# Low parts of a weight piece's sums in one operation, sums made ahead in three operations, and two norms' roots moved into the softmax

## The chip, the cores and the metric

The kernel runs on one core of a Trainium2 chip. The core's engines run side by side, each one through its own instructions in their order: TensorE (PE: matmuls; PEld: its weight loads), VectorE (DVE), ScalarE (ACT), GpSimd (POOL) and SyncE (SP). An instruction waits by semaphores for what other engines or DMA transfers must have finished. The metric is the time of one execution in device microseconds (us); lower is better.

## What is computed

The reference is one layer of a streaming encoder in float32, on 256 tokens with 2048 features. Cut to its frame:

```python
x = x + 0.5 * swiglu(rms_norm(x, ffn1_norm[l]), ffn1_w_up[l], ffn1_w_down[l])
h = rms_norm(x, mix_norm[l]); proj = h @ w_in[l]
...                                   # HGRN2 and RG-LRU branches, gates, w_out
x = x + cross_attention(rms_norm(x, xattn_norm[l]), rms_norm(mem, mem_norm[l]), wq, wkv, wo)
x = x + 0.5 * swiglu(rms_norm(x, ffn2_norm[l]), ffn2_w_up[l], ffn2_w_down[l])
return rms_norm(x, final_norm)

def swiglu(h, w_up, w_down):
    gate, up = jnp.split(h @ w_up, 2, axis=-1)
    return (jax.nn.silu(gate) * up) @ w_down
```

In the cross attention, 4 heads of 512 features attend to 256 memory tokens: scores = q k^T * 512^-0.5, softmax over the memory tokens, times v, then wo. An RMS norm multiplies a token's row by 1/sqrt(mean of squares + eps), here called its root, and each feature by a gain. The root of a token is one number for the whole row, so it can be applied before or after a product with a weight. The feed-forward width is 5632, so each of the two feed-forward parts reads an up weight of 2048 x 11264 and a down weight of 5632 x 2048.

## The kernel before

**Pieces.** All weights come as pieces of 128 x 2048 numbers (1 MB). SP issues the load of a piece into a tile `raw`; the products read it as a high part and a low part, both in the reduced form that TensorE multiplies fast. `split` (L137 to L139) makes them: ScalarE copies the piece to the high part `h`, and VectorE subtracts that from the piece, which gives the low part `l`. The activations are split in the same way (`xh`, `xl`). A product then consists of three: h by xh (L547), h by xl (L548) and l by xh (L550, in the function `three`). In a feed-forward piece all h matmuls come ahead of the l matmuls.

**Fewer matmuls by sums.** For most up pieces (kind "fast") the kernel multiplies sums of the four 128x512 blocks of a piece in place of some of the blocks, so that 7 products do the work of 8. In `prepare`, VectorE makes the sums `td` from `raw`: one operation of 128x1024 (L285), then one of 128x512 (L287) and one more (L288), each of which needs the one before. The blocks that are used as they are get split as 128x1536 (`h`, `l`), and `td` gets split into `th` and `tl` in two halves of 1024 columns: two ScalarE copies (L138) and two VectorE subtractions (L139, 128x1024). In the first feed-forward part `td` and `tl` lie in a pool `wide` of three tiles; in the second `td` lies in a tile of the raw pools (so the profile shows it as raw), and `tl` in `wide`, of two tiles.

Other kinds are "fast added" (the low part of the 1536 columns is made by a ScalarE copy with the sign turned and a POOL DMA that adds the weight to it, L293 to L295), "added" (the same for a whole piece, L254 to L263), "plain" (one split of 128x2048), and "ready": there `td` isn't computed but loaded from a tile `t` in DRAM.

**Sums made ahead.** For the "ready" pieces of the second feed-forward part, 58 of them, `make_ahead` (L191 to L202) runs in the middle of the kernel: POOL issues the load of the piece into `prep`, VectorE makes the sums in place with four subtractions of 128x512 (L200), and POOL issues the store to `t`. `beside` (called for every piece) says after which piece the next such load, or its sums and store, are put into the instruction stream.

**Order.** The stages follow each other: first feed-forward part (up to about 690 us in the profile), input projection and branches, gates and output (up to about 1356), q and k of the cross attention, scores, v and o (up to about 1740), second feed-forward part (up to 2417). A feed-forward cycle is 8 up pieces, and 4 down pieces of an earlier group; between them stand the activation (L580, L581) and transposes (L588) that give `hidop`, the operand of the down pieces. `weights` prepares two pieces ahead of the one in use; pools of three raw, three h and three l tiles limit how far that goes (a new load waits until the last reader of the tile is done). The order of the instructions within each engine is decided by a scheduler when the kernel is built: it simulates the engines and places what is ready. Only the first eight pieces have an order written by hand. So a change in an operation's cost or form can also change the order of other instructions.

**Norms of q and k.** In the loop over q's 16 tiles (L1088), `summed` (L347 to L355) adds the two partial results of a product (L352) and, where `by=` is given, multiplies the sum by a [128, 256] tile (L354). For q that tile is `by_feature(sq3.rstd_tokens())`: the roots as a column per token are turned into a row by two VectorE products with the identity, one matmul with ones, and one ScalarE copy; then it is scaled by 512^-0.5. For k it is `rmem` (L1105), which comes from `sqm.rstd()`. `scores` (L1110) multiplies q and k (L1118, L1119), adds the parts, takes the maximum over the memory tokens (L1122), turns its sign (L1123), and lets ScalarE take Exp with that as bias and the sum as a second result (L1124).

Of the kernel before, what the change touches and what calls it, by code (L numbers as in the profile page):

```python
# [8 lines left out]
F32 = mybir.dt.float32  # L9
F32R = mybir.dt.float32r  # L10
ACT = mybir.ActivationFunctionType
ALU = mybir.AluOpType

P = 128
# [8 lines left out]
HD = D // HEADS  # L23
# [54 lines left out]
def block_kernel(ctx: ExitStack, tc: tile.TileContext, xT, xin, memT, vec, gfin, bgate, lruw, wu1, wd1, win, wv,  # L78
                 wg, wab, wout, wq, wk, wvm, wo, wu2, wd2, out_):
    nc = tc.nc  # L80
    pe, dve, act, sp = nc.tensor, nc.vector, nc.scalar, nc.sync
# [23 lines left out]
    def slot(dt=F32, name="slot"):  # L105
        return slots.tile([P, 1024], dt, name=name, tag="slot")

    def t1(name="t1"):
        return scoped["tmp"].tile([P, T], F32, name=name, tag="t1")

    def bank(name="acc"):
        return psum.tile([P, 512], F32, name=name, tag="acc")
# [18 lines left out]
    x = [xt[k // 4][:, (k % 4) * T:(k % 4 + 1) * T] for k in range(KT)]  # L131
    ident = col("ident", 0, P)

    done = {}


    def split(h, l, raw):  # L137
        done["high"] = act.activation(h, raw, ACT.Copy).ins  # L138
        done["low"] = dve.tensor_tensor(out=l, in0=raw, in1=h.bitcast(F32), op=ALU.subtract).ins  # L139

    def split_tiles():
        return hp.tile([P, 2048], F32R, name="h", tag="h"), lp.tile([P, 2048], F32R, name="l", tag="l")
# [49 lines left out]
    def make_ahead(src, to):  # L192

        t = scoped["prep"].tile([P, 2048], F32, name="prep", tag="prep")
        nc.gpsimd.dma_start(t, src)
        yield
        b = [t[:, i * 512:(i + 1) * 512] for i in range(4)]
        with tc.issue_after(done["low"]):
            for o, x, y in ((1, 0, 1), (0, 0, 2), (2, 2, 1), (3, 3, 2)):
                dve.tensor_tensor(out=b[o], in0=b[x], in1=b[y], op=ALU.subtract)  # L200
        nc.gpsimd.dma_start(to, t)
        yield  # L202

# [39 lines left out]
    def raw_tile():  # L243

        if "raw2" in scoped and next(loads) % 5 > 2:
            return scoped["raw2"].tile([P, 2048], F32, name="raw2", tag="raw2")
        return rawp.tile([P, 2048], F32, name="raw", tag="raw")
# [10 lines left out]
    def prepare(src, kind, cuts=1):  # L258

        if kind == "added":  # L260
            raw, l = begun.pop(0)
            h = hp.tile([P, 2048], F32R, name="h", tag="h")
            done["high"] = act.activation(h, raw, ACT.Copy).ins  # L263
            return h, l
        raw = raw_tile()
        n = 2048 // cuts
        if kind == "plain":
            h, l = split_tiles()
            for a in range(0, 2048, n):
                sp.dma_start(raw[:, a:a + n], src[:, a:a + n])  # L270
                split(h[:, a:a + n], l[:, a:a + n], raw[:, a:a + n])
            return h, l
        if kind == "ready":
            src, t = src
            sp.dma_start(raw[:, 512:], src[:, 512:])
            td = raw_tile()
            sp.dma_start(td, t)
        else:
            sp.dma_start(raw, src)
            if "raw2" in scoped:  # L280
                td = raw_tile()
            else:
                td = scoped["wide"].tile([P, 2048], F32, name="td", tag="wide")
            two = [v[:, a:a + 1024].rearrange("p (i n) -> p i n", i=2) for v, a in ((td, 0), (raw, 512))]
            dve.tensor_tensor(out=two[0], in0=raw[:, None, :512].broadcast_to([P, 2, 512]), in1=two[1],  # L285
                              op=ALU.subtract)
            dve.tensor_tensor(out=td[:, 1024:1536], in0=raw[:, 1024:1536], in1=td[:, :512], op=ALU.subtract)  # L287
            dve.tensor_tensor(out=td[:, 1536:], in0=raw[:, 1536:], in1=td[:, 1024:1536], op=ALU.subtract)  # L288
        h, l = split_tiles()
        if kind != "fast added":  # L290
            split(h[:, 512:], l[:, 512:], raw[:, 512:])
        else:
            act.activation(l[:, 512:], raw[:, 512:], ACT.Copy, scale=-1.0)  # L293
            nc.gpsimd.dma_start(l[:, 512:], src[:, 512:], accum_op=ALU.add)
            done["high"] = act.activation(h[:, 512:], raw[:, 512:], ACT.Copy).ins  # L295
        th = hp.tile([P, 2048], F32R, name="h", tag="h")
        if "wide" in scoped:
            tl = scoped["wide"].tile([P, 2048], F32R, name="tl", tag="wide")
        else:
            tl = lp.tile([P, 2048], F32R, name="tl", tag="l")  # L300
        for a in (0, 1024):
            split(th[:, a:a + 1024], tl[:, a:a + 1024], td[:, a:a + 1024])
        return (h, l), (th, tl)

    def product(xs, *ws, late=()):
# [41 lines left out]
    def summed(acc, out=None, by=None):  # L347

        lo = t1("lo")
        act.activation(lo, acc[:, T:], ACT.Copy)  # L350
        out = t1("sum") if out is None else out
        dve.tensor_tensor(out=out, in0=acc[:, :T], in1=lo, op=ALU.add)  # L352
        if by is not None:
            dve.tensor_tensor(out=out, in0=out, in1=by, op=ALU.mult)  # L354
        return out  # L355
# [103 lines left out]
    def by_feature(r):  # L459

        diag = t1("diag")
        for t in range(2):
            dve.tensor_scalar(out=diag[:, t * P:(t + 1) * P], in0=ident, scalar1=r[:, t:t + 1], scalar2=None,
                              op0=ALU.mult)
        acc = bank()
        pe.matmul(acc[:, :T], ones, diag, start=True, stop=True)
        o = small.tile([P, T], F32, name="rstd", tag="rstd", bufs=2)
        act.activation(o, acc[:, :T], ACT.Copy)
        return o
# [310 lines left out]
    def heads(t):  # L780
        return t.rearrange("p (h t) -> p h t", h=4)
# [291 lines left out]
    xs3, sq3 = Operands(), TokenSquares()  # L1073
# [12 lines left out]
    qs = Operands()  # L1086
    ms, sqm = Operands(), Squares()
    for m in range(KT):  # L1088
        acc = two_ahead(xs3.tiles, "q", m, 0, late)
        if m == 0:  # L1090
            rstd = by_feature(sq3.rstd_tokens())
            dve.tensor_scalar(out=rstd, in0=rstd, scalar1=HD ** -0.5, scalar2=None, op0=ALU.mult)
        qs.add(summed(acc, by=rstd))
        for i in range(2 * m, 2 * m + 2) if m < 4 else (m + 4,) if m < 12 else ():
            if i % 4 == 0:
                mt = slot(name="mem")
                sp.dma_start(mt, memT[:, i * T:(i + 4) * T])
            mk = heads(mt)[:, i % 4]
            ms.add(mk, col("mem_norm", i))
            sqm.add(mk)  # L1100
    ks = Operands()
    for m in range(KT):
        acc = two_ahead(ms.tiles, "k", m, 0)
        if m == 0:
            rmem, rmtok = sqm.rstd(), sqm.rstd_tokens()  # L1105
        ks.add(summed(acc, by=rmem))

    probs = {}

    def scores(h):  # L1110
        p = slot(name="p")
        pv = p.rearrange("p (t m) -> p t m", t=4)
        for t in range(2):
            acc = bank()
            for j in range(4):
                d = h * 4 + j
                a, b = t * P, T + t * P
                pe.matmul(acc, qs.tiles[d][:, a:a + P], ks.tiles[d], start=(j == 0), stop=False)  # L1118
                pe.matmul(acc[:, :T], qs.tiles[d][:, b:b + P], ks.tiles[d][:, :T], start=False, stop=(j == 3))  # L1119
            s = summed(acc, out=pv[:, t])  # L1120
            st = small.tile([P, 4], F32, name="st", tag="st", bufs=4)
            dve.tensor_reduce(out=st[:, 0:1], in_=s, axis=mybir.AxisListType.X, op=ALU.max)  # L1122
            dve.tensor_scalar(out=st[:, 1:2], in0=st[:, 0:1], scalar1=-1.0, scalar2=None, op0=ALU.mult)  # L1123
            act.activation(s, s, ACT.Exp, bias=st[:, 1:2], accum_out=st[:, 2:3])  # L1124
            dve.reciprocal(out=st[:, 3:4], in_=st[:, 2:3])
            dve.tensor_scalar(out=s, in0=s, scalar1=st[:, 3:4], scalar2=None, op0=ALU.mult)
            yield
        acc = bank()
        for mt in range(2):
            for t in range(2):  # L1130
                pe.transpose(acc[:, mt * T + t * P:][:, :P], pv[:, t, mt * P:(mt + 1) * P], ident)
        ps = slot(F32R, "ps")
        psv = ps.rearrange("p (m t) -> p m t", m=2)
        av = acc.rearrange("p (m t) -> p m t", m=2)
        act.activation(psv[:, :, :T], av, ACT.Copy)
        dve.tensor_tensor(out=psv[:, :, T:], in0=av, in1=psv[:, :, :T].bitcast(F32), op=ALU.subtract)
        probs[h] = ps
        yield
# [3 lines left out]
    for g in range(4):  # L1142
# [4 lines left out]
        for t in range(2):  # L1147
            s = slot(F32R, "vs")
# [8 lines left out]
    for h in range(HEADS):  # L1157
        for j in range(4):
            acc = bank()
            for t in range(2):  # L1160
                ps = probs[h][:, t * 512:(t + 1) * 512]
                s = vs[h, t]
# [153 lines left out]
```

## Time and profile before

| | us |
|---|---|
| median of 3 runs | 2428.28 |
| lowest and highest run | 2426.31 and 2430.49 |
| span of the profiled execution | 2425.5 |

No separate time is given for the profiled execution, so its span is the only number for it; it lies 2.8 us below the median.

How to read the profile's rows: a group row holds the line, engine, operation, what it writes and reads with shapes, and the count; then busy time and mean duration of one (ns), then the idle time of the engine right before these instructions and what ended it. A timeline row holds start and duration in us, engine, line, operation, names and shapes, a count where several follow each other, and in brackets the idle time before it with the releaser. A row of waits holds the waiting instruction, what it waited for, and the total, the number and the longest of the waits. A row of the chain holds start and duration of a step of the work that ended last. In a row of a window, after the stretch and its length, come the busy time of PE, PEld, DVE, ACT and POOL with their counts, the clock that TensorE was granted (1.00 is full), the share of the DMA engines and GB/s. Matmuls are pipelined: the records of two in a row overlap, so a matmul's record is longer than the step from one to the next.

### The profile page before, as it was taken

To read this page: it belongs to the slowest core of one execution; us is meant where nothing else is said; L and a number is where in the kernel's file an instruction comes from. 1 tells how busy PE (TensorE), PEld (TensorE's weight loads), DVE (VectorE), ACT (ScalarE), POOL (GpSimd) and SP (SyncE) were. 2 spreads that over 40 slices of the span, in tenths; PEclk is the share of its full clock that TensorE was granted. 3 is DMA by queue.
4 is the path that set the end of the run, shared out by engine and by line. 5 is a ranking of instruction groups with operands and counts; after the bars stand their busy time and mean duration, and the time that the engine had idled before them with its cause. 6 is when DMAs were issued, how large, how long until landed. Compare 5 with 4: busy or idle time off the path is not lost.

```text
span 2425.5 us, 30763 instructions
## 1 busy us (share of the span) xinstructions
PE 2409.3 (99%) x12139; PEld 2013.6 (83%) x12139; DVE 2025.6 (84%) x2260; ACT 1455.0 (60%) x1485; POOL 102.2 (4%) x166
## 2 busy tenths in 40 slices
PE   9999999999999999999999999999999999999998
PEld 8888888888788888888888888888888788888887
DVE  7999999998876868779776788777789999999995
ACT  8567677777664454476434555445676666666664
POOL 0000000000000000000000000000000000000000
PEclk9999999999999999999999999999999999999999
DMA  7579999988858776778989889977798878787873
GB/s 294 195 229 287 272 272 270 275 269 268 266 183 323 268 289 241 294 289 323 346 313 349 310 332 354 335 272 263 264 343 308 285 266 293 273 286 276 294 273 144
DMA packets 102385, 684.31 MB, mean 282 GB/s; under 512 B 11361, under 2 KB 11617, under 8 KB 29281
## 3 DMA queue, kind: packets, MB, share of 16 engines
q1 hardware_dynamic: 78192, 518.68, 57.5%
q0 software_dynamic: 23328, 162.54, 22.4%
q8 instruction: 95, 1.56, 0.2%
q10 hardware_dynamic: 720, 1.13, 0.1%
q14 instruction: 50, 0.40, 0.0%
HBM read 619.39 MB, written 62.91 MB: 281 GB/s over the span
## 4 chain that ended last, share of the span: by engine, by line
PE 91%; DVE 3%; DMA 3%; ACT 1%; issue 1%; ACTq 0%; DVEq 0%; SPq 0%
PE acc L547 16%; PE acc L548 16%; PE acc L550 16%; PE acc L313 11%; PE acc L338 8%; PE acc L341 8%; PE acc L339 8%; PE acc L316 6%; DMA raw<-wd 2%; DVE tl L139 1%; ACT h L138 1%; DVE l L139 1%; PE acc L588 1%; PE acc L477 1%; DMA t<-prep 0%
## 5 line engine op out<-in xcount | busy, mean ns | idle before, releaser
L138 ACT ACTIVATE h<-raw 128x2048 fp32r<-128x2048 f32 (+3 forms) x578 | 870.5, 1531 | 620.2 <-PE acc L339 189.6
L139 DVE TENSOR_TENSOR l<-raw,h 128x2048 fp32r<-128x2048 f32 (+2 forms) x406 | 837.3, 2065 | 187.6 <-ACT h L138 186.1
L547 PE MATMUL acc<-h,xh 128*128 128x512 f32 x1241 | 485.2, 392 | 2.7 <-ACT h L138 2.4
L548 PE MATMUL acc<-h,xl 128*128 128x512 f32 x1241 | 483.0, 390 | 0.0
L338 PE MATMUL acc<-h,ops 128*128 128x512 f32 x832 | 326.8, 393 | 0.0
L339 PE MATMUL acc<-h,ops 128*128 128x512 f32 x832 | 324.5, 390 | 0.0
L547 PEld LDWEIGHTS acc<-h,xh 128*128 128x128 f32 x1241 | 233.3, 188 | 56.2 <-ACT h L138 8.0
L547 PE MATMUL acc<-h,hidop 128*128 128x512 f32 x704 | 276.5, 393 | 2.3 <-ACT h L138 2.2
L313 PE MATMUL acc<-ops,h 128*128 128x512 f32 x1152 | 278.2, 393 | 0.0
L548 PE MATMUL acc<-h,hidop 128*128 128x512 f32 x704 | 274.8, 390 | 0.0
L548 PEld LDWEIGHTS acc<-h,xl 128*128 128x128 f32 x1241 | 233.3, 188 | 47.5
L313 PEld LDWEIGHTS acc<-ops,h 128*128 128x128 f32 x1152 | 211.7, 188 | 41.6
L139 DVE TENSOR_TENSOR tl<-raw,h 128x1024 fp32r<-128x1024 f32 x172 | 203.7, 1220 | 14.9 <-ACT h L138 14.5
L341 PE MATMUL acc<-l,ops 128*128 128x512 f32 x832 | 205.8, 389 | 0.0
L550 PE MATMUL acc<-l,hidop 128*128 128x512 f32 x704 | 189.3, 389 | 0.0
L138 ACT ACTIVATE h<-td 128x1024 fp32r<-128x1024 f32 x126 | 131.3, 1057 | 92.9 <-PE acc L548 42.3
L341 PEld LDWEIGHTS acc<-l,ops 128*128 128x128 f32 x832 | 156.2, 188 | 32.4
L338 PEld LDWEIGHTS acc<-h,ops 128*128 128x128 f32 x832 | 156.2, 188 | 32.2
L339 PEld LDWEIGHTS acc<-h,ops 128*128 128x128 f32 x832 | 156.3, 188 | 31.5
L139 DVE TENSOR_TENSOR tl<-td,h 128x1024 fp32r<-128x1024 f32 x126 | 152.0, 1220 | 31.2 <-ACT h L138 31.0
L200 DVE TENSOR_TENSOR prep<-prep 128x512 f32<-128x512 f32 x232 | 159.7, 689 | 20.9 <-DMA prep<-wu 17.1
L550 PE MATMUL acc<-l,xh 128*128 128x512 f32 x645 | 176.4, 389 | 0.0
(242 smaller groups left out, 2739.4 us busy)
## 6 DMA issues: line engine op xcount, KB each, us to landing
raw<-wu SPq DMA_DIRECT2D x114, 1024.0 KB, 6.3
raw<-wd SPq DMA_DIRECT2D x88, 1024.0 KB, 6.3
prep<-wu POOLq DMA_DIRECT2D x58, 1024.0 KB, 7.8
t<-prep POOLq DMA_DIRECT2D x58, 1024.0 KB, 7.8
raw<-t SPq DMA_DIRECT2D x58, 1024.0 KB, 6.9
raw<-wu SPq DMA_DIRECT2D x58, 768.0 KB, 5.0
raw<-win SPq DMA_DIRECT2D x40, 1024.0 KB, 4.8
raw<-wg SPq DMA_DIRECT2D x32, 1024.0 KB, 6.1
```

The costliest lines, as they stand in the source:

```text
L138: done["high"] = act.activation(h, raw, ACT.Copy).ins
L139: done["low"] = dve.tensor_tensor(out=l, in0=raw, in1=h.bitcast(F32), op=ALU.subtract).ins
L200: dve.tensor_tensor(out=b[o], in0=b[x], in1=b[y], op=ALU.subtract)
L313: pe.matmul(acc, h[:, k * P:(k + 1) * P], xs[k], start=k == 0, stop=False)
L316: done["product"] = pe.matmul(acc[:, :T], l[:, k * P:(k + 1) * P], xs[k][:, :T], start=False, stop=k == KT - 1).ins
L338: pe.matmul(accs[t], x[:, t * P:][:, :P], h[j], start=first and j == 0, stop=False)
L339: pe.matmul(accs[t], x[:, T + t * P:][:, :P], h[j], start=False, stop=False)
L341: done["product"] = pe.matmul(accs[t], x[:, t * P:][:, :P], l[j], start=False, stop=last and j == 3).ins
L477: pe.transpose(acc[:, z * T + t * P:][:, :P], tile[:, t * 512 + (2 * y + z) * P:][:, :P], ident)
L547: pe.matmul(acc, ah, bh, start=start, stop=False)
L548: pe.matmul(acc, al, bh, start=False, stop=False)
L550: pe.matmul(acc, ah, bl, start=False, stop=stop)
```

## The change

1. The sums' low part: `td` is still copied to `th` in two halves by ScalarE, but `tl` comes from one VectorE subtraction of 128x2048 in place of two of 128x1024. It needs both halves of `th`. This holds for every piece with sums, 149 in all.
2. The sums made ahead: the first two of the four subtractions become one of 128x(2x512), whose first operand is block 0, read twice, whose second operand is blocks 1 and 2, and whose results go to blocks 1 and 0, in that order. Two of 128x512 follow. This holds for the 58 pieces made ahead.
3. The roots: q's and k's tiles are no longer multiplied by anything. q's root with 512^-0.5 stays a column per token, and is used as the scale of Exp and in the product that makes its bias; `by_feature` isn't called. k's root `rmem` multiplies each score tile (8 of them, 128x256).

```diff
@@ -194,10 +194,12 @@
         t = scoped["prep"].tile([P, 2048], F32, name="prep", tag="prep")
         nc.gpsimd.dma_start(t, src)
         yield
-        b = [t[:, i * 512:(i + 1) * 512] for i in range(4)]
+        b = t.rearrange("p (i n) -> p i n", i=4)
         with tc.issue_after(done["low"]):
-            for o, x, y in ((1, 0, 1), (0, 0, 2), (2, 2, 1), (3, 3, 2)):
-                dve.tensor_tensor(out=b[o], in0=b[x], in1=b[y], op=ALU.subtract)
+            dve.tensor_tensor(out=b[:, 1::-1], in0=b[:, :1].broadcast_to([P, 2, 512]), in1=b[:, 1:3],
+                              op=ALU.subtract)
+            for o in (2, 3):
+                dve.tensor_tensor(out=b[:, o], in0=b[:, o], in1=b[:, o - 1], op=ALU.subtract)
         nc.gpsimd.dma_start(to, t)
         yield
 
@@ -299,7 +301,8 @@
         else:
             tl = lp.tile([P, 2048], F32R, name="tl", tag="l")
         for a in (0, 1024):
-            split(th[:, a:a + 1024], tl[:, a:a + 1024], td[:, a:a + 1024])
+            done["high"] = act.activation(th[:, a:a + 1024], td[:, a:a + 1024], ACT.Copy).ins
+        done["low"] = dve.tensor_tensor(out=tl, in0=td, in1=th.bitcast(F32), op=ALU.subtract).ins
         return (h, l), (th, tl)
 
     def product(xs, *ws, late=()):
@@ -1088,9 +1091,9 @@
     for m in range(KT):
         acc = two_ahead(xs3.tiles, "q", m, 0, late)
         if m == 0:
-            rstd = by_feature(sq3.rstd_tokens())
-            dve.tensor_scalar(out=rstd, in0=rstd, scalar1=HD ** -0.5, scalar2=None, op0=ALU.mult)
-        qs.add(summed(acc, by=rstd))
+            rtok = sq3.rstd_tokens()
+            dve.tensor_scalar(out=rtok, in0=rtok, scalar1=HD ** -0.5, scalar2=None, op0=ALU.mult)
+        qs.add(summed(acc))
         for i in range(2 * m, 2 * m + 2) if m < 4 else (m + 4,) if m < 12 else ():
             if i % 4 == 0:
                 mt = slot(name="mem")
@@ -1103,7 +1106,7 @@
         acc = two_ahead(ms.tiles, "k", m, 0)
         if m == 0:
             rmem, rmtok = sqm.rstd(), sqm.rstd_tokens()
-        ks.add(summed(acc, by=rmem))
+        ks.add(summed(acc))
 
     probs = {}
 
@@ -1117,11 +1120,12 @@
                 a, b = t * P, T + t * P
                 pe.matmul(acc, qs.tiles[d][:, a:a + P], ks.tiles[d], start=(j == 0), stop=False)
                 pe.matmul(acc[:, :T], qs.tiles[d][:, b:b + P], ks.tiles[d][:, :T], start=False, stop=(j == 3))
-            s = summed(acc, out=pv[:, t])
+            s = summed(acc, out=pv[:, t], by=rmem)
             st = small.tile([P, 4], F32, name="st", tag="st", bufs=4)
             dve.tensor_reduce(out=st[:, 0:1], in_=s, axis=mybir.AxisListType.X, op=ALU.max)
-            dve.tensor_scalar(out=st[:, 1:2], in0=st[:, 0:1], scalar1=-1.0, scalar2=None, op0=ALU.mult)
-            act.activation(s, s, ACT.Exp, bias=st[:, 1:2], accum_out=st[:, 2:3])
+            r = rtok[:, t:t + 1]
+            dve.tensor_scalar(out=st[:, 1:2], in0=st[:, 0:1], scalar1=r, scalar2=-1.0, op0=ALU.mult, op1=ALU.mult)
+            act.activation(s, s, ACT.Exp, bias=st[:, 1:2], scale=r, accum_out=st[:, 2:3])
             dve.reciprocal(out=st[:, 3:4], in_=st[:, 2:3])
             dve.tensor_scalar(out=s, in0=s, scalar1=st[:, 3:4], scalar2=None, op0=ALU.mult)
             yield
```

## The prediction

> **What bounds the kernel now.** I read the page's first part, the chain of work, then the waits of TensorE, the windows by stage and, where a wait stands, the timeline around it.
>
> ```profile
> span 2425.5 us, 30763 instructions
> PE 2409.3 (99%) x12139; PEld 2013.6 (83%) x12139; DVE 2025.6 (84%) x2260; ACT 1455.0 (60%) x1485; POOL 102.2 (4%) x166
> PE 91%; DVE 3%; DMA 3%; ACT 1%; issue 1%; ACTq 0%; DVEq 0%; SPq 0%
> ```
>
> ```profile
> 11.14 1.81 PE acc L550 x8
> ```
>
> The chain is TensorE for 91%. Its matmuls of 512 columns follow each other at 1.81 / 8 = 0.2265 us, so nothing is won inside its work, only in its gaps. The waits put those in few places:
>
> ```profile
> PE acc L547 <- ACT h L138: 4.6, 5, 2.0
> ...
> PE acc L892 <- DVE k L912: 0.9, 1, 0.9
> ```
>
> Five waits for a high part cost 4.6 us; they all stand where a feed-forward cycle passes from its last up piece to its first down piece. (From start to start a gap is some 0.16 us longer than its idle time, since a matmul's record outlasts its turn.) VectorE is second, and close to full in the feed-forward parts:
>
> ```profile
> 60.00:250.00 190.00, 190.00 (x850) 156.89 (x849) 182.10 (x190) 122.55 (x102) 6.74 (x8) 1.00 0.74 239
> 1905.00:1930.00 25.00, 22.40 (x89) 17.07 (x88) 22.57 (x22) 17.75 (x14) 0.88 (x1) 0.93 0.81 300
> ```
>
> The columns are PE, PEld, DVE, ACT and POOL, then TensorE's clock. From 60 to 250 VectorE has 182 of 190 us and TensorE still never waits. In the second row TensorE loses 2.6 us to waits, and 7% of 25 us = 1.75 us to a lower clock.
>
> **The change: VectorE's work.**
>
> ```profile
> L139 DVE TENSOR_TENSOR l<-raw,h 128x2048 fp32r<-128x2048 f32 x269 | 615.3, 2288 | 184.3 <-ACT h L138 182.9 <-DMA xf<-xT 1.1
> L139 DVE TENSOR_TENSOR tl<-raw,h 128x1024 fp32r<-128x1024 f32 x172 | 203.7, 1220 | 14.9 <-ACT h L138 14.5
> L200 DVE TENSOR_TENSOR prep<-prep 128x512 f32<-128x512 f32 x232 | 159.7, 689 | 20.9 <-DMA prep<-wu 17.1
> L139 DVE TENSOR_TENSOR tl<-td,h 128x1024 fp32r<-128x1024 f32 x126 | 152.0, 1220 | 31.2 <-ACT h L138 31.0
> L354 DVE TENSOR_TENSOR sum<-sum,rstd 128x256 f32<-128x256 f32 x56 | 23.5, 421 | 0.6
> ```
>
> Of the low parts, 172 + 126 = 298 operations become 149 of 128x2048. By durations a pair saves 2 x 1220 - 2288 = 152 ns, 23 us in all. Back to back it saves less, as records overlap:
>
> ```profile
> 1909.56 3.49 DVE L139 TENSOR_TENSOR tl<-raw,h 128x1024 fp32r<-128x1024 f32 x3
> 1001.47 4.50 DVE L139 TENSOR_TENSOR l<-raw,h 128x2048 fp32r<-128x2048 f32 x2 [3.24 <-ACT h L138]
> ```
>
> Three small ones take 3.49 us, a step of (3.49 - 1.22) / 2 = 1.135; two large ones 4.50, a step of 4.50 - 2.29 = 2.21. A pair then saves 2 x 1.135 - 2.21 = 0.06 us. I take 0.07 us a pair, since VectorE is mostly queued here: about 10 us.
>
> [...]
>
> The sums made ahead go from 4 operations to 3 in 58 places; a 128x(2x512) operation is priced by 1220, so 4 x 0.689 - (1.22 + 2 x 0.689) = 0.16 us each, 9 us. The reversed order of its two outputs is in no row: between 0 (as an ordinary 128x1024) and, run as two operations, +0.16 each, no saving; I take the first, as its operands are otherwise those of ordinary ones. For q and k, 32 multiplies of 0.42 us go, 13 us, and 8 come on the scores. All of this lies beside TensorE: cost and gain nothing, except where VectorE is late.
>
> **By_feature.** Removed are one matmul with ones and its two scalings.
>
> ```profile
> L940 PE MATMUL acc<-osq,ones x16: 377/379/380, 905.7 to 1049.1; 128*128 128x256 f32 x16
> ...
> 1554.50 0.27 DVE L1123 TENSOR_SCALAR st<-st 128x1 f32<-128x1 f32 x2
> ...
> 1556.53 1.28 ACT L1124 ACT_TABLE_LOAD   x1
> ```
>
> The like matmul at L940 appears as two records each; at their turn of about 0.215 us that is **-0.43 us**, on the path. The extra multiply of the scores (0.42 us each, two ahead of the first Exp) ends near 1555.6, when ScalarE still has its h and then the table load to 1557.81: hidden. If that cover goes, 0.8 us.
>
> **The low part comes later.** The one operation can start only when ScalarE has both high halves. Before, the first half's subtraction filled that time:
>
> ```profile
> 246.80 2.44 DVE L139 TENSOR_TENSOR tl<-td,h 128x1024 fp32r<-128x1024 f32 x2
> ...
> 246.92 1.06 ACT L138 ACTIVATE h<-td 128x1024 fp32r<-128x1024 f32 x1 [0.26 <-DVE td L288]
> ...
> 251.93 0.84 PE L550 MATMUL acc<-tl,xh 128*128 128x512 f32 x3
> ```
>
> Here tl was whole at 249.24. In one operation it would start at 247.98 + 0.04 and end at 250.31: 1.07 us later, with 1.1 us idle on VectorE. TensorE takes it at 251.93, so 1.6 us are left. In the order in which the changed kernel issues, 36 of the 149 follow their last sum (L288) directly; others have an l of 1.75 or 2.29 us between, which covers the wait. VectorE's idle time so made, 36 x 1.1 = 40 us at most, is more than the 19 us saved, but not in the stretch 60 to 250, where nearly all have an l between.
>
> **Cycle ends of the first feed-forward part.** Seven ends; three of them:
>
> ```profile
> 253.10 1.92 ACT L138 ACTIVATE h<-raw 128x2048 fp32r<-128x2048 f32 x1 [1.55 <-DMA raw<-wd]
> ...
> 255.10 0.39 PE L550 MATMUL acc<-l,xh 128*128 128x512 f32 x1
> ...
> 256.01 0.50 PE L547 MATMUL acc<-h,xh 128*128 128x512 f32 x1 [0.53 <-ACT h L138]
> ```
>
> ```profile
> 317.37 0.39 PE L550 MATMUL acc<-l,xh 128*128 128x512 f32 x1
> 317.90 0.50 PE L547 MATMUL acc<-h,xh 128*128 128x512 f32 x1
> ...
> 625.62 1.92 ACT L138 ACTIVATE h<-raw 128x2048 fp32r<-128x2048 f32 x1 [2.25 <-DMA raw<-wd]
> ...
> 626.48 0.39 PE L550 MATMUL acc<-l,xh 128*128 128x512 f32 x1
> ...
> 628.53 0.50 PE L547 MATMUL acc<-h,xh 128*128 128x512 f32 x1 [1.66 <-ACT h L138]
> ```
>
> TensorE waits for the last piece's second high half, which ScalarE makes after the first down piece's h, which waited for its DMA (at 317.90, right after its last sum). The gaps are 0.91 - 0.23 = 0.69, 0.53 - 0.23 = 0.30 and 2.05 - 0.23 = 1.83; the other four are of the kind of the 0.30 and smaller, by my estimate 0.2 each. ScalarE keeps its order; TensorE's changes. It now does the rest of l (2 x 0.23) and then five matmuls of the down piece (1.13 us) before that half. The h is ready at 255.02 and 627.54; TensorE comes to it at 255.78 and 627.16: gaps of 0 and 0.4. So 3.6 us become 0.4: **-3.2 us**. What is late next is tl, but twelve hidop matmuls and four of l stand before it.
>
> **Cycle ends of the second part.** One is heavy:
>
> ```profile
> 1916.37 1.22 DVE L139 TENSOR_TENSOR tl<-raw,h 128x1024 fp32r<-128x1024 f32 x1
> 1916.42 0.85 PE L550 MATMUL acc<-l,xh 128*128 128x512 f32 x3
> 1917.50 0.69 DVE L288 TENSOR_TENSOR raw<-raw,raw 128x512 f32<-128x512 f32 x1
> 1918.45 4.66 ACT L138 ACTIVATE h<-raw 128x2048 fp32r<-128x2048 f32 x3 [1.00 <-DMA raw<-wd]
> 1920.41 0.50 PE L547 MATMUL acc<-h,hidop 128*128 128x512 f32 x1 [2.04 <-ACT h L138]
> 1921.91 0.63 PE L547 MATMUL acc<-h,xh 128*128 128x512 f32 x1
> ```
>
> ```profile
> 1910.80 7.57 DMA raw<-wd
> ```
>
> Here the DMA of wd decides. SP issued it at 1910.80, when VectorE's tl operations (the row at 1909.56) let go of a raw tile. Six pairs merged earlier in the cycle bring that forward by 6 x 0.07 = 0.4 us. Moreover the half tl that stood ahead of L288 goes behind it: L288 ends 1.13 + 0.4 earlier, near 1916.65, the second high half near 1917.7, tl near 1920.0. TensorE would wait 0.6 us for the half and 1.4 for tl, and go on to hidop at 1920.9; before, the same work (four matmuls of the half, two of tl, 1.36 us) would have it there at 1921.77: **-0.8 us**. And after 2.04 us of idleness a matmul took 0.63 us instead of 0.39 (1921.91); the clock's loss is the 1.75 us above. After 1.66 us idle at 628.53 it did not fall. With waits of 0.6 and 1.4 it should not: **-1.7 us**.
>
> [...]
>
> ```profile
> 1981.34 2.86 ACT L138 ACTIVATE h<-raw 128x2048 fp32r<-128x2048 f32 x2 [3.02 <-DMA raw<-wd]
> 1983.31 0.50 PE L547 MATMUL acc<-h,hidop 128*128 128x512 f32 x1 [0.19 <-ACT h L138]
> ```
>
> ```profile
> 2348.06 0.61 PE L550 MATMUL acc<-tl,xh 128*128 128x512 f32 x2
> ...
> 2348.73 0.50 PE L547 MATMUL acc<-h,hidop 128*128 128x512 f32 x1
> ```
>
> At 1983.31 the gap is 0.19 + 0.16 = 0.35, at 2348.73 it is 0.67 - 2 x 0.2265 = 0.22. The second half now comes before this h, in time that ScalarE spent idle (3.02 us), and TensorE reaches the down piece 0.45 us later: that gap goes, and the other likewise: **-0.6 us**. In the other seven ends, tl or the down piece's l would be in time by only about 0.8 us; I put **+0.8 us** there, between 0 and 7 x 1.07 = 7.5.
>
> **Sum.** -3.2 - 0.8 - 1.7 - 0.6 - 0.4 + 0.8 = -5.9 on the profiled span of 2425.5, so 2419.6. The median is 2.8 us above that span, with no other time given for the profiled execution; so **2422.4 us**. Nothing else moves: the POOL and SP queues keep their instructions and order, the middle's one wait (0.9 us for k, VectorE blocked by a DMA) stays.
>
> **Rivals.**
> *The waits only change name.* DMA landings and ScalarE's order set the ends; the halves trade one wait for another. For it: the h at 253.10, 625.62 and 1918.45 all follow a DMA. Then only 0.4 of the ones matmul and 0.6 come: 2427.2.
> *Slower: the late low part.* In the second part's ten ends tl directly after its last sum is 1.07 us late against 0.8 of margin, VectorE idles, and what comes next (l, the release of raw, the next wd load) slips too. It decides once an end loses 0.6 us more than it has margin (10 x 0.6 = 5.9). At 0.8 us and with the clock still falling once or twice (1.7 each), and half of the first part's gain kept: 8 + 1.7 - 1.6 = +8: 2436. For it: VectorE 84% busy, 22.57 of 25 us at the heavy end. Against: 60 to 250, where TensorE never waits at 96% VectorE.
> *VectorE is the bound after all*, and 10 + 9 + 10 us come through: 2399. Against it: PE 91% of the chain.
>
> **How the numbers follow.** About 0.2%, 4.9 us, is what can be told from no change. Forecast 0.45 (0.37 below 2423.4, the rest above; its own range 2418 to 2426); waits renamed 0.27; slower 0.25; VectorE 0.03. Faster 0.40, same 0.35, slower 0.25. The range 2418 to 2437 leaves out the last rival and the far ends of the others.
>
> **What would show it.** After: tl rows of 2.29 us, 149 in all, with VectorE idle 1.1 us ahead of some; the waits for ACT h under 2 us in sum; the clock 1.00 in every window; PE records down by two. Wrong, if a wait of L550 for tl appears many times, or the half clock at several cycle ends.

## The result: slower by 2.7%, nearly all of it lost in the first feed-forward part

The changed kernel takes **2492.77 us** (median of 5 runs, 2484.93 to 2501.22) against 2428.28 us before (5 runs): a ratio of **1.0272**, 95% interval 1.0249 to 1.0294. The forecast was 2422.4 us.

The profiled execution after is the quickest of its five (2484.93 us, span 2483.2 us). The head of its page, and the chain of work by engine:

```profile
span 2483.2 us, 30577 instructions
PE 2431.7 (98%) x12137; PEld 2008.3 (81%) x12137; DVE 2007.4 (81%) x2027; ACT 1452.1 (58%) x1484; POOL 102.2 (4%) x166
PE 78%; DVE 8%; DMA 5%; ACT 4%; issue 4%; ACTq 0%; DVEq 0%; SPq 0%; POOLq 0%
```

VectorE has 18 us less to do, as it should, and yet the chain has moved away from TensorE: VectorE, ScalarE and DMA now make up 17% of it, where they made up 7%. The transposes that follow the cycles (L588 before, L591 after) divide the kernel. In each kernel, these rows are the last ones of the first feed-forward part, the first of the second part, and the last:

```profile
648.01 1.03 PE L588 MATMUL acc<-vt,ev 128*128 128x128 f32 x8
...
1784.05 0.27 PE L588 MATMUL acc<-vt,hid 128*128 128x128 f32 x1
...
2366.82 1.03 PE L588 MATMUL acc<-vt,hid 128*128 128x128 f32 x8
```

```profile
703.46 1.03 PE L591 MATMUL acc<-vt,ev 128*128 128x128 f32 x8
...
1839.44 0.28 PE L591 MATMUL acc<-vt,hid 128*128 128x128 f32 x1
...
2424.50 1.03 PE L591 MATMUL acc<-vt,hid 128*128 128x128 f32 x8
```

At 648 us the changed kernel is 55.4 us late. The middle takes as long as before (1135.98 against 1136.04 us), and the second part is 2.3 us longer. So of this execution's 57.7 us, 96% arise in the first part. The waits of TensorE after (total, times, longest) show what they are:

```profile
PE acc L550 <- ACT h L304: 17.2, 18, 1.7
PE acc L553 <- DVE tl L305: 11.0, 16, 1.3
PE acc L550 <- ACT h L138: 7.2, 16, 0.6
```

L304 is the copy of the sums' halves, L305 the low part in one operation. Before, the waits for a high part had 4.6 us in all and those for tl 0.4. Up to the transposes at 703.46 us TensorE stands idle for 36.3 us, against 3.6 us up to those at 648.01 before; the rest of the 55.4 us (the longer turns around each gap, stretches at a lower clock) is not split up here. Here is one stretch of the first part after, VectorE's timeline and then ScalarE's:

```profile
389.99 2.29 DVE L305 TENSOR_TENSOR tl<-td,h 128x2048 fp32r<-128x2048 f32 x1 [1.55 <-ACT h L304]
392.20 1.22 DVE L287 TENSOR_TENSOR td<-raw 128x1024 f32<-128x1024 f32 x1
393.45 0.69 DVE L289 TENSOR_TENSOR td<-raw,td 128x512 f32<-128x512 f32 x1
394.18 0.69 DVE L290 TENSOR_TENSOR td<-raw,td 128x512 f32<-128x512 f32 x1
396.94 2.29 DVE L305 TENSOR_TENSOR tl<-td,h 128x2048 fp32r<-128x2048 f32 x1 [2.08 <-ACT h L304]
```

```profile
393.53 1.06 ACT L304 ACTIVATE h<-td 128x1024 fp32r<-128x1024 f32 x1 [2.20 <-DVE td L287]
394.50 1.47 ACT L297 ACTIVATE h<-raw 128x1536 fp32r<-128x1536 f32 x1
395.87 1.04 ACT L304 ACTIVATE h<-td 128x1024 fp32r<-128x1024 f32 x1
400.47 1.06 ACT L304 ACTIVATE h<-td 128x1024 fp32r<-128x1024 f32 x1 [3.55 <-DVE td L287]
```

It is a ring. The low part (389.99) holds VectorE for 2.2 us; only behind it does the next piece's first sum begin (392.20); only then can ScalarE copy the first half (393.53), then an h of another 1536 columns that its order puts between, then the second half (395.87 to 396.91); and only then can the next low part start (396.94). One turn takes 2.21 + 1.33 + 0.97 + 1.37 + 1.07 = 6.95 us, and VectorE stands still for 2.08 of it, ScalarE for 2.20 (and for 3.55 in the turn behind it). TensorE needs 21 x 0.2265 = 4.76 us for the 21 matmuls of such a piece. So TensorE waits for the ring wherever several such pieces follow each other.

The rest of the loss, from 57.7 us in the profiled execution to 64.5 in the median, comes together with lower clocks: the five runs had mean granted clocks of 0.997, 0.995, 0.996, 0.991 and 0.993 for 2484.93, 2492.77, 2487.44, 2501.22 and 2497.8 us. One thousandth of 2490 us is 2.5 us.

### The profile page after: what moved, and what is told of

It reads as the page before. It is cut to its first block, busy times and chain, and to the rows that moved or that the text cites. A ratio compares the mean times of both kernels' runs of the same rounds, so it can differ in the third digit from the quotient of the medians.

```text
span 2483.2 us, 30577 instructions
## 1 busy us (share of the span) xinstructions
PE 2431.7 (98%) x12137; PEld 2008.3 (81%) x12137; DVE 2007.4 (81%) x2027; ACT 1452.1 (58%) x1484; POOL 102.2 (4%) x166
## 3 DMA queue, kind: packets, MB, share of 16 engines
q10 hardware_dynamic: 720, 1.13, 0.1%
## 4 chain that ended last, share of the span: by engine, by line
PE 78%; DVE 8%; DMA 5%; ACT 4%; issue 4%; ACTq 0%; DVEq 0%; SPq 0%; POOLq 0%
PE acc L550 13%; PE acc L553 13%; PE acc L551 13%; PE acc L316 10%; PE acc L344 7%; PE acc L341 7%; PE acc L342 7%; PE acc L319 5%; DVE tl L305 3%; DVE l L139 2%; DMA raw<-wu 2%; ACT h L138 2%; DVE td L287 1%; DMA l<-wu 1%; ACT h L304 1%
## 5 line engine op out<-in xcount | busy, mean ns | idle before, releaser
L138 ACT ACTIVATE h<-raw 128x2048 fp32r<-128x2048 f32 (+2 forms) x406 | 702.0, 1733 | 510.6 <-PE acc L342 204.5
L304 ACT ACTIVATE h<-raw 128x1024 fp32r<-128x1024 f32 x172 | 174.6, 1054 | 136.5 <-PE acc L551 79.5
L305 DVE TENSOR_TENSOR tl<-raw,h 128x2048 fp32r<-128x2048 f32 x86 | 196.1, 2288 | 30.4 <-ACT h L304 30.2
L304 ACT ACTIVATE h<-td 128x1024 fp32r<-128x1024 f32 x126 | 132.5, 1052 | 144.2 <-DVE td L287 129.2
L305 DVE TENSOR_TENSOR tl<-td,h 128x2048 fp32r<-128x2048 f32 x63 | 144.2, 2288 | 46.8 <-ACT h L304 45.9
```

Of the source, the lines that this page charges most:

```text
L304: done["high"] = act.activation(th[:, a:a + 1024], td[:, a:a + 1024], ACT.Copy).ins
L305: done["low"] = dve.tensor_tensor(out=tl, in0=td, in1=th.bitcast(F32), op=ALU.subtract).ins
```

## The experiments

Theory A: the ring above, that is, the wait for both halves together with the next sums behind it. Rival B: one operation of 2.29 us holds VectorE or its tile too long. Rival C: the other two parts of the change. Rival D: the pool of three tiles for sums and low parts. All results are ratios to the kernel before, measured in turn on the same chip.

**E1 leaves out the first part of the change.**

```diff
-            done["high"] = act.activation(th[:, a:a + 1024], td[:, a:a + 1024], ACT.Copy).ins
-        done["low"] = dve.tensor_tensor(out=tl, in0=td, in1=th.bitcast(F32), op=ALU.subtract).ins
+            split(th[:, a:a + 1024], tl[:, a:a + 1024], td[:, a:a + 1024])
```

> The change without its first part: sums made ahead in three and the roots moved, the low part in two operations as before. If the low part in one operation is the cause of the loss (theory A: it waits for both high halves, and VectorE stands there with the next piece's sums queued behind it), this is 2422 to 2430 us. If the sums made ahead or the roots cost something (rival C), it is above 2440.

Measured: 2434.45 us (10 runs, 2425.02 to 2442.39), ratio 1.0029, interval 1.0013 to 1.0044. So nearly the whole loss goes with the first part; but the time lies 4 us above theory A's range, so there is a second, small loss that neither theory had (E5).

**E2 keeps the one operation only where `"raw2" in scoped`, in the second feed-forward part.**

> The change, but with the low part in one operation in the second feed-forward part alone (its first part keeps two). Theory A, by the cycles of the profile after (55.4 us of the loss lie ahead of 703 us, 2.3 us in the second part): 2424 to 2433 us. If the second part only looks unharmed because it follows a late first part: above 2440.

Measured: 2434.08 us (7 runs), ratio 1.0036, interval 1.0024 to 1.0049. Like E1: in the second part the one operation does no harm that these times could tell (in the profile TensorE waits there 5.3 us for tl, in eight places).

**E3 makes two operations that both come after the second half.**

```diff
-        done["low"] = dve.tensor_tensor(out=tl, in0=td, in1=th.bitcast(F32), op=ALU.subtract).ins
+        second = dve.tensor_tensor(out=tl[:, 1024:], ...).ins        # needs the second half of th
+        with tc.issue_after(second):
+            done["low"] = dve.tensor_tensor(out=tl[:, :1024], ...).ins
```

> The low part in two operations again, but the second half first, and the first half's queued behind it on VectorE: so both come after the second high half, without being one operation. Theory A (the wait for both halves is what costs): as the change, 2480 to 2505 us, as VectorE does the same in the same order. Rival B (one operation of 2.29 us blocks VectorE or releases its tile too coarsely): 2425 to 2440 us.

Measured: 2491.01 us (4 runs, 2488.57 to 2491.91), ratio 1.0269, interval 1.0252 to 1.0286: the same as the change, without any operation of 2.29 us. So the one operation as such is not the cause; that VectorE is held for 2.28 us in a row is the same here, and E4 shows that this alone costs no more than 0.9 us in the first part: rival B falls. VectorE's timeline of E3 has the same standstill ahead of two small operations, and the same turn of the ring, 395.58 - 388.55 = 7.03 us:

```profile
388.55 1.23 DVE L305 TENSOR_TENSOR tl<-td,h 128x1024 fp32r<-128x1024 f32 x1 [1.13 <-ACT h L304]
389.69 1.22 DVE L307 TENSOR_TENSOR tl<-td,h 128x1024 fp32r<-128x1024 f32 x1
390.83 1.22 DVE L287 TENSOR_TENSOR td<-raw 128x1024 f32<-128x1024 f32 x1
...
395.58 1.22 DVE L305 TENSOR_TENSOR tl<-td,h 128x1024 fp32r<-128x1024 f32 x1 [2.08 <-ACT h L304]
```

**E4 keeps the one operation, but puts it behind the next piece's first sum in the first part.**

```diff
+        waiting.append(<the low part's operation>)     # issued by the next piece's prepare
...
+            first = dve.tensor_tensor(out=two[0], ...).ins          # the next piece's first sum
+            with tc.issue_after(first):
+                while waiting: waiting.pop(0)()
```

> The change, but in the first feed-forward part each low part is issued behind the next piece's first sum (L285) instead of ahead of it. Theory A (the loss is the next sums queued behind the waiting low part): VectorE's wait stays but ScalarE gets its halves earlier; most of the loss goes, 2430 to 2450 us. If the three tiles of the pool that holds sums and low parts bind instead (rival D), the next sums can't start earlier and it stays at 2480 us or more.

Measured: 2439.92 us (4 runs), ratio 1.0061, interval 1.0041 to 1.0080. Its first part ends at 648.93 us, 0.9 us after that of before: of 55.4 us, 54.5 are gone, by order alone, with the same three tiles. Rival D falls, and theory A stands. VectorE's waits between 250 and 690 us, before, in the changed kernel and in E4 (L305 became L314 there, L304 L312):

```profile
DVE tl L139 <- ACT h L138: 28.2, 17, 2.1
DVE l L139 <- ACT h L138: 8.6, 7, 3.1
```

```profile
DVE tl L305 <- ACT h L304: 38.7, 20, 2.4
DVE l L139 <- ACT h L138: 30.1, 26, 1.6
```

```profile
DVE tl L314 <- PE acc L564: 15.2, 11, 2.6
DVE l L139 <- ACT h L138: 7.3, 7, 3.1
DVE tl L314 <- ACT h L312: 6.5, 6, 1.1
```

VectorE waited for the halves before too, 28.2 us, and TensorE hardly noticed; the length of this wait is not what decides. What the ring adds is ScalarE's wait for the next piece's first sum, in the same stretch, in the same three kernels:

```profile
ACT h L138 <- DVE td L285: 17.1, 14, 1.3
```

```profile
ACT h L304 <- DVE td L287: 90.8, 33, 4.3
```

```profile
ACT h L312 <- DVE td L292: 9.2, 6, 1.5
```

Theory A had expected VectorE's wait for the halves to stay and to harm nothing. Most of it went as well, from 38.7 to 6.5 us: the next sums now fill it. In its place the low part waits 15.2 us for TensorE, most likely for a tile of the pool of rival D, and that costs nothing that shows: TensorE's waits from 60 to 690 us add up to 2.4 us in E4 and to 2.2 before.

**E5, E6 and E7 make one part of the change each:** the sums made ahead in three; the roots; the one operation.

> The second part of the change alone: sums made ahead in three operations. E1 came out 0.3% slower than before with one wait of 9.6 us for VectorE's k near 812 us, behind sums made ahead that waited for their load. If the three operations move VectorE into that wait (theory E), this is 2429 to 2437 us, and its profile shows a wait of TensorE for k of several us. If it is the load's own timing, which falls either way in any kernel (rival F), or the roots (rival G): 2423 to 2428 us.

> The third part alone: the roots moved. By the sum of the prediction -0.4 us: 2424 to 2428 us. Rival G (the roots carry e1's loss): 2430 us or more.

> The first part alone: the low part in one operation, everywhere. By e3 and the result it carries nearly the whole loss: 2478 to 2495 us. If the loss needs the other parts too, it is well below, under 2465 us.

| part alone | median us, runs | ratio (95%) |
|---|---|---|
| E5, sums made ahead in three | 2432.19, 12 | 1.0019 (1.0007 to 1.0031) |
| E6, roots | 2424.29, 11 | 0.9994 (0.9985 to 1.0002) |
| E7, low part in one operation | 2492.46, 4 | 1.0278 (1.0262 to 1.0294) |

The parts account for the change. The 0.4 us foreseen for E6 can't be told from nothing. E5 is a small loss, but clear of noise, and E1 and E2, which have its three operations too, lose 0.29 and 0.36%. Its runs spread from 2425.53 to 2438.67 us, and its profile has this (VectorE twice, then TensorE):

```profile
740.38 1.23 DVE L199 TENSOR_TENSOR prep<-prep 128x1024 f32<-128x1024 f32 x1 [6.45 <-DMA prep<-wu]
...
779.75 1.23 DVE L199 TENSOR_TENSOR prep<-prep 128x1024 f32<-128x1024 f32 x1 [9.31 <-DMA prep<-wu]
```

```profile
808.78 1.08 PE L873 MATMUL acc<-silu,k 128*32 128x32 f32 x64 [7.44 <-DVE k L858]
```

The first operation of 128x(2x512) takes 1.23 us where an ordinary one of 128x1024 takes 1.22: its reversed output costs nothing. But VectorE stands ahead of it until the piece has landed in the only `prep` tile of this stage, and the k that TensorE wants comes 7.4 us late, behind that. The sums' waits for their load add up, in the profiles, to 34.8 us in E5, 36.8 in E1, 28.4 in E2, 30.9 in E4, against 17.1 before, 14.5 in E6 and 17.1 in E8 (below), which have four operations. It isn't so in every execution: the changed kernel's own profile has 18.2 us and E3's 20.6, both with three operations and a late first part, and E7's has 20.7 with four, and a wait of TensorE for that k of 4.2 us. So three operations make this wait longer or more frequent, but four don't rule it out.

**E8 adds the one operation in the second part to the roots, with four sums made ahead.**

> The roots, and the low part in one operation in the second feed-forward part alone; the sums made ahead in four. If theory E holds, the losses of the other parts are left out, and the gain predicted for the second part (3 us at its cycle ends, 0.4 us for the ones matmul) can show: 2420 to 2425 us. If the late low part costs as much there as its cycle ends gain: 2425 to 2429 us.

Measured: 2426.73 us (11 runs), ratio 1.0000, interval 0.9992 to 1.0009. The order foreseen for the heavy cycle end is there, but little of the gain is the change's, and it is lost again elsewhere. The window of 1905 to 1930 us of E8, and in it VectorE, ScalarE and TensorE (L304 is the one operation, L303 the second half's copy):

```profile
1905.00:1930.00 25.00, 23.66 (x102) 18.58 (x101) 22.81 (x20) 18.18 (x15) 0.89 (x1) 1.00 0.88 307
```

```profile
1915.46 0.69 DVE L288 TENSOR_TENSOR raw<-raw,raw 128x512 f32<-128x512 f32 x1
...
1916.18 1.06 ACT L303 ACTIVATE h<-raw 128x1024 fp32r<-128x1024 f32 x1 [1.85 <-DVE raw L288]
...
1917.28 2.29 DVE L304 TENSOR_TENSOR tl<-raw,h 128x2048 fp32r<-128x2048 f32 x1 [1.13 <-ACT h L303]
...
1919.62 1.20 PE L555 MATMUL acc<-tl,xh 128*128 128x512 f32 x4 [1.13 <-DVE tl L304]
```

The last sum comes earlier, TensorE waits 1.13 us for tl and no longer for the down piece's h, and the clock stays at 1.00. But the clock stays at 1.00 in E5 too, which has two operations here as before and TensorE's old wait (a window around that end, then TensorE's timeline):

```profile
1915.00:1940.00 25.00, 22.41 (x96) 17.38 (x95) 22.78 (x22) 19.03 (x16) 0.88 (x1) 1.00 0.82 304
```

```profile
1930.67 0.50 PE L549 MATMUL acc<-h,hidop 128*128 128x512 f32 x1 [2.02 <-ACT h L138]
```

So the half clock at this end (0.53 from 1921.3 to 1924.9 us before) doesn't come with a wait of that length in every profile. From the first matmul with hidop of the cycle end ahead (1868.28 us before) to the first one behind the next transposes (1940.65), the kernel before takes 72.37 us, E8 71.52, and E5 70.74. And in the whole second part TensorE now waits 4.2 us for low parts, in five places: this one, and four others, where up pieces 9 us and more ahead of the down pieces are multiplied (1.50 us at 1898.96, inside the stretch just measured, is the longest).

**E9 puts a fourth operation behind E5's three** (`b[:, 3] = max(b[:, 3], b[:, 3])`), so that the store of the sums doesn't come earlier.

> E5 with a fourth VectorE operation of 128x512 behind the three (it changes no value), so that the store of the sums waits for as long as before, and VectorE's time is no less than before. In e5's profile the first store starts 1.2 us earlier (724.15 against 725.32), beside SP's loads of wv, and takes longer; the next load lands later, and VectorE waits 6.45 us for it where it waited 1.86. If this earlier store is the cause (theory E2): 2424 to 2429 us, like before. If the form of the first operation or its place in VectorE's order is (rival): 2430 to 2436 us, like e5.

Measured: 2430.76 us (9 runs, 2429.12 to 2433.36), ratio 1.0025, interval 1.0015 to 1.0035. In its profile the first wait shrinks as expected, from 6.45 to 2.52 us, but others come later (27.8 us in eight places), and the k is still 3.4 us late. So the earlier store is not the cause, or not the whole of it; nor is a shorter time of VectorE's work. What is left is the form of the first operation, or the place that the order gives these operations against their loads. Neither was tried, and the cause of this small loss stays open.

**E10 and E12 look for a version that beats both:** the roots, and the one operation only in the 58 pieces whose sums are loaded (E10), or only in the last up piece of each cycle of the second part (E12).

> The roots, and the low part in one operation only in the 58 pieces whose sums are loaded (both high halves follow each other on ScalarE, and no sum of VectorE's stands ahead of the second). E8 gave 0.0%, with 4.2 us of waits for the low part. If those waits come from pieces with sums made on the spot: 2420 to 2425 us. If any late low part costs as much as it saves in the second part: 2425 to 2429 us.

> The roots, and the low part in one operation only in the last up piece of each of the second part's ten cycles that have sums, where the down pieces' load follows. In e8's profile the heavy end (1905 to 1930 us) lost 1.34 us to waits at clock 1.00, where before lost 2.60 at 0.93; but TensorE waited 4.2 us for low parts, mostly in other pieces. If the gain at the ends is real and the loss lies in the other pieces: 2420 to 2424 us. If the order of VectorE shifts elsewhere with it: 2424 to 2429 us.

Measured: E10 2429.08 us (11 runs), ratio 1.0012, interval 1.0003 to 1.0021; E12 2424.93 us (12 runs), ratio 0.9996, interval 0.9986 to 1.0005. E10's profile shows no wait for tl, but one of 3.7 us for a low part that a POOL DMA completes: the loss of that execution comes elsewhere. In E12 TensorE's waits of the second part are 2.1 us in all, and the stretch that took 72.37 us before and 70.74 in E5 takes 70.21; still E12 can't be told from E6, which has the roots alone. So no version measured here beats the kernel before clearly.

**E11 is E4 with four sums made ahead.**

> E4 with the sums made ahead in four operations as before: the low part in one operation everywhere, in the first part behind the next piece's first sum, and the roots. E4 stood 14 us over before, of which its first part had under 1 us. If the two losses add (e5 is 5.5 us of it): 2428 to 2435 us. If the middle's loss comes from the order of the first part: 2436 us or more.

Measured: 2431.11 us (11 runs), ratio 1.0020, interval 1.0012 to 1.0029. This is within the range that the sum of the parts gave. In the profile the wait of several us for k is gone (1.4 us), it enters the second part 0.9 us after the kernel before, and what is left arises there, where TensorE waits for low parts (5.2 us for tl, in six places).

## Why the prediction was wrong

- **VectorE's work: right in kind, and worth nothing.** The low parts are 149 rows of 2288 ns, and VectorE's busy time fell by 18.2 us (10 + 9 + 10 foreseen). No run gained by it; the rival in which VectorE is the bound is out.
- **The step that failed is "The low part comes later".** It had the delay right for one piece (1.07 us; 1.6 us of margin in TensorE) and it counted a piece at a time. What stands behind the waiting operation on VectorE was left out: the next piece's sums, from which ScalarE's next halves come, from which the next low part comes. A delay that comes back as the start of the next piece isn't covered once by a margin; it sets a period. (The many waits of TensorE for tl that the prediction named as the sign of being wrong came: 16, beside 18 for a high half.) The rows for that period were there: low part 2.29, first sum 1.22, two copies of 1.06 and, between them, an h of 1.48 (the mean of the 128x1536 copies before) make 7.1 us, against 4.76 us of TensorE. Before, the ring was open: the first half's subtraction ran during ScalarE's second copy, and the next piece's first sum could stand between the halves, as in these rows of VectorE before:

```profile
360.18 1.22 DVE L139 TENSOR_TENSOR tl<-td,h 128x1024 fp32r<-128x1024 f32 x1
361.31 1.22 DVE L285 TENSOR_TENSOR td<-raw 128x1024 f32<-128x1024 f32 x1
362.45 1.22 DVE L139 TENSOR_TENSOR tl<-td,h 128x1024 fp32r<-128x1024 f32 x1
```

  E3 (same wait, no merge) and E4 (same merge, other order) show that this is the cause.
- **"From 60 to 250 nearly all have an l between" didn't protect.** By the transposes at 213 us before, 10.6 us were lost already: the l waits for its own h on ScalarE, which comes late in the same ring.
- **Cycle ends of the first part: -3.2 us foreseen, not seen in the changed kernel.** The order foreseen came, the gain did not: everything ahead of these ends was late, and TensorE waited in 16 places, up to 0.6 us, for an h that is split whole. In E4, where the ring is undone, the gain can be seen: it reaches the transposes of 213.19 us before at 217.30, and those of 648.01 at 648.93, so it wins 3.2 us in between. But the size rested in part on luck, there too. The two large gaps, at 256.01 and 628.53 us, aren't in every execution: E2's first part has two operations as before, and there the view of TensorE's waits from 60 to 690 us is empty.
- **Cycle ends of the second part: the order right, two terms wrong.** At the heavy end the half comes first and TensorE waits 1.13 us for tl (1.4 foreseen), as E8 shows. The term of -1.7 us for the clock was read from one execution: in E5, with two operations there as before, TensorE waits 2.02 us at this end and the clock stays at 1.00 (1915 to 1940 us). Against E5, the one operation at this end is worth 70.74 - 70.21 = 0.5 us in E12, of the 0.8 foreseen. And the +0.8 us for the other ends stood in the wrong place and was too small: E8 waits for tl at none of them, but for 3.0 us in four other places, where the sum had put nothing. The sum was -3.1 + 0.8; what was measured for E8 is 0.0% with the roots in it.
- **"Nothing else moves" was wrong.** The sums made ahead cost 0.19% (0.07 to 0.31), and longer waits of VectorE for their load go with it in E5. That these operations are in a ring too, with POOL's store and load, and that a change in their number shifts VectorE against it, is a reading that no run shows.
- **The rival "the late low part" had the sign and the operation, and the wrong place.** It put 8 us at the second part's ends; the loss was 55 us in the first part's pieces, where sums made on the spot put VectorE and ScalarE in series. Why the second part, of whose 86 pieces with sums 58 have them loaded, loses so little was not tested by itself.
- **The ones matmul:** TensorE's records fell by two (12139 to 12137), as foreseen; 0.4 us is below what E6 can tell.

## What to carry to other kernels

When an operation is merged so that it waits for the later of two producers, write down what stands behind it on its engine, and follow that around until it comes back to the producer; if it does, compare the period of the ring with the bound engine's time for a piece (6.95 against 4.76 us here), not the delay with the margin of one piece (1.07 against 1.6). A saving on an engine that is off the critical path was no gain by itself (18.2 us of VectorE here), and the waiting that came with it put more of that engine on the path (3% of the chain before, 8% after). Where a merged operation must stay, issuing the next piece's independent work ahead of it gave back 54.5 of 55.4 us in the first part here. And a gap seen in one profiled execution is not yet a gap in every execution: TensorE's waits of 0.53 and 1.66 us at the first part's ends, and the half clock in the second, were absent from the profiles of E2 and E5, which are the same there.

## What the runs showed of the hardware that was not expected

The prediction held waits of 0.6 and 1.4 us to be too short for a fall of the clock, since it had fallen after 2.04 us and not after 1.66. In the changed kernel it is down at 264.5 us, after waits of 0.69 and 1.09 us (TensorE's timeline, then a window; the clock is the last column but two):

```profile
261.93 1.19 PE L553 MATMUL acc<-tl,xh 128*128 128x512 f32 x4 [0.69 <-DVE tl L305]
264.21 0.79 PE L550 MATMUL acc<-h,xh 128*128 128x512 f32 x1 [1.09 <-ACT h L304]
```

```profile
264.50:266.50 2.00, 2.00 (x5) 1.53 (x5) 0.94 (x1) 1.98 (x2) 0.00 (x0) 0.50 0.47 90
```

At 172 us it falls (0.50 from 172 to 174 us) after waits of 1.69 and 0.61 us, in a stretch (168 to 172 us) in which TensorE was busy for 1.70 of 4 us. So here the clock fell behind shorter waits that stand close together, too; and the clocks of the five runs (0.991 to 0.997) and their times go together. Nor does the length of the longest wait decide it: behind 1.66 us at 628.53 us before, the clock stayed at 1.00 (628.5 to 632 us), and behind 1.09 us in the rows above it was 0.50; at the second part's heavy end a wait of 2.04 us before was followed by 0.53 (1921.3 to 1924.9 us), and one of 2.02 us in E5 was not followed by any fall (1.00 from 1915 to 1940 us). What decides it was not shown.
